# Multi-query attention on one core: last sum of VectorE's exponentials as accumulating DMAs of GpSimd, query loads by quarters of half batches, transpositions of 4096 columns

## The chip, the cores and the metric

One core of a Trainium2 chip. The core's engines are named as the profile names them: PE (TensorE, matmuls), ACT (ScalarE), DVE (VectorE), POOL (GpSimd), SP (SyncE, which here issues DMAs alone). Times are device microseconds (us). The metric is the time of one execution; the profile adds one execution's span and its instructions.

## The reference

```python
batch, seq_len, embed_dim = (8, 1024, 1024)
num_heads = 16
head_dim = embed_dim // num_heads          # 64
# q: (8, 1024, 16, 64)   k, v: (8, 1024, 64), all float32
q = q.transpose(0, 2, 1, 3)
scores = np.matmul(q, k.transpose(0, 1, 3, 2)) / np.sqrt(head_dim)
weights = np.exp(scores - np.max(scores, axis=-1, keepdims=True))
weights = weights / np.sum(weights, axis=-1, keepdims=True)
attn_out = np.matmul(weights, v)           # back to (8, 1024, 16, 64)
```

The 16 heads of a batch share its keys and values. The kernel takes no maximum off: it takes exponentials of the scaled scores and divides at the end by their sum, which a column of ones beside the values yields.

## The kernel before

**Tiles.** Work goes by pairs of heads: 8 batches x 8 pairs = 64 pairs (`NP`). Each pair has 8 tiles (`NKT`), one per 128 keys: a tile holds the scores of 128 keys against 1024 queries of two heads, so 128 x 2048. There are 512 tiles. Scores come in two halves of 512 queries, 128 x 1024 in float32, in one of three PSUM slots. `score` (L369) makes a half with two matmuls out of the transposed keys `k2t` and the transposed queries `qt`.

**Exponentials.** Most halves go to ACT: `exp_act` (L384), one instruction for 128 x 1024, written as fp16 into the weight tile `wt` (28 buffers). The other tiles go to DVE, by `exp_dve` (L389): two instructions (L396, one a half) turn the scores into 16-bit integers `z`, which read as fp16 are a first approximation of the exponential; then six steps over all 2048 columns refine it with a polynomial of the mantissa bits:

1. `f` = `z` and 1023 (L411)
2. `m` = (`f` - 1024) / 1024 (L413)
3. a linear factor out of `f`, kept in `wt` (L416)
4. `m` = `f` x `m` (L419)
5. `wt` = `m` x `wt`, the correction (L420)
6. `wt` = `z` + `wt`, as integers (L421)

**Values.** `value` (L424) multiplies a weight tile, as 128 x 128 stationary blocks, with the values of its 128 keys and a column of ones. The 16 blocks of a pair are in three groups (`GROUPS`), each summed over its 8 tiles in a PSUM bank; `reciprocal` and `normalise` (L443, L448) divide by the sum on DVE and issue the store of a pair on SP.

**Order.** `plan` (L50) lays out all instructions of PE, ACT and DVE in one list ahead of time, with a price for each kind of instruction and a due time for each tile. It decides which tiles are DVE's (a new one is taken when the DVE work in its list is under `BACKLOG`), and when the values of a tile can be multiplied. `LAG` says how many pairs the value matmuls stay behind the scores, `LAST` how many of the last tiles DVE takes none of. The three engines run in exactly that order; each waits, in its order, for what it needs. SP's and POOL's queues are not in the list: a scheduler orders them when the kernel is built, and each runs its own queue in order.

**Loads.** POOL loads the queries of a pair with a cast to fp16 (`load_q`, L307: 128 partitions x 8 runs of 128 elements, runs of 512 B at the source) into `qn` (4 buffers), keys and values a batch ahead (`load_k`, `load_v`). SP transposes by DMA: 1024 columns a pair (`trans_q`, L317) into `qt` (3 buffers), and the doubled keys of a batch (`trans_k`, L300). `begin(w)` (L469) issues these when the scores of pair w begin: the load of pair w+3, the transposition of pair w+2, and the next batch's keys at the third and values at the fifth pair of a batch. A load waits until the buffer that it overwrites has been transposed; a transposition waits until PE has made the last scores out of the `qt` buffer it overwrites. The first pair of all is loaded, cast and turned by other engines (`load_first`, `cast_first`, `turn_first`).

Of the kernel before, what the change touches and what calls it, by code (L numbers as in the profile page):

```python
# [9 lines left out]
FP32 = mybir.dt.float32  # L10
FP16 = mybir.dt.float16
U16 = mybir.dt.uint16
EXP = mybir.ActivationFunctionType.Exp
ALU = mybir.AluOpType
ENG = mybir.EngineType

P = 128
ONE = 1024.0
GA = 0.30457565
# [5 lines left out]
END, END_LAG, B_END = 5.0, 0.0, 5.0  # L25
VEC = dict(z=1.13, rec=0.11, norm=0.44)
STEPS = (0.6, 0.6, 0.6, 1.13, 1.13, 1.13)
VEC_L = 0.19
VEC_DEP = 0.12
GROUPS = ((0, 6), (6, 11), (11, 16))  # L30
# [1 line left out]
PITCH = 68  # L32
BACKLOG, BACK_END, BACK_LAST = 5.5, 3.0, 6.0
FIRST, DVE_0 = 4, 2.3
LAST = 12
WBUFS = 28
LAG = 1.8
FAR = 1e9

def follows(x, y):  # L40
# [9 lines left out]
def plan(NP, NKT):  # L50
# [28 lines left out]
    while p < NP or groups:  # L79
# [113 lines left out]
        else:  # L193
# [8 lines left out]
            if z:  # L202
                x = z[0]
                zs.remove(x)
                r, s, u = x
                T = max(T, r)
                emit(T, "z", *u)
                dve = T + VEC["z"]
                slot[s] = dve + VEC_L
                if u[1] == 1:  # L210
                    steps += [(u[0], n) for n in range(len(STEPS))]
                last = ("z", u[0])
            elif what == "ev":
                evs.remove(x)
                _, ep, eg, a, k = x
                emit(T + late, k, ep, eg)
                dve = T + late + VEC[k]
                if k == "norm":
                    acc[a] = dve + VEC_L
                last = x  # L220
            elif what == "step":
                steps.remove(x)
                emit(T + late, "step", *x)
                dve = T + late + STEPS[x[1]]
                if x[1] == len(STEPS) - 1:
                    ready[x[0]] = dve + VEC_L
                last = x
            else:
                nxt = [x[0] for x in zs + evs if x[0] > T] + [pe + 1e-6] * (pe > T)
                dve = max(min(nxt, default=0.0), T + 1e-3)  # L230
                last = None
# [6 lines left out]
def kernel(  # L238
# [12 lines left out]
    NQC = S // QC  # L251
    HT = NKT // NQC
    HP = H // 2
    NP = B * HP
    VW = 72
    vscale = ONE / (math.log(2.0) * math.sqrt(D))
# [17 lines left out]
    qt: dict = {}  # L274
    sc: dict = {}
    wt: dict = {}
    zs: dict = {}
    steps: dict = {}
    acc: dict = {}
    rec: dict = {}  # L280
# [2 lines left out]
    def load_k(b):  # L283

        st = kst.setdefault(b, {})
        st["k16"] = kvp.tile([P, NKT, 2, D], FP16, tag="k16", name=f"k16{b}")
        for r in range(2):
            nc.gpsimd.dma_start(  # L288
                out=st["k16"][:, :, r, :], in_=k[b].rearrange("(c p) d -> p c d", p=P)
            )  # L290

    def load_v(b):
        st = kst[b]
        st["v"] = kvp.tile([P, NKT, VW], FP16, tag="v", name=f"v{b}")
        nc.gpsimd.dma_start(  # L295
            out=st["v"][:, :, 0:D], in_=v[b].rearrange("(c p) d -> p c d", p=P)
        )
        nc.gpsimd.memset(st["v"][:, :, D : D + 1], 1.0)

    def trans_k(b):  # L300
# [3 lines left out]
            out=st["k2t"], in_=st["k16"].rearrange("p c r d -> p (c r d)")  # L304
        )

    def load_q(p):  # L307
        if p >= NP or p in qn:
            return
        b, hp = divmod(p, HP)  # L310
        qn[p] = qp.tile([P, NKT, 2 * D], FP16, tag="qn", name=f"qn{p}")
        nc.gpsimd.dma_start(  # L312
            out=qn[p],
            in_=q[b, :, 2 * hp : 2 * hp + 2, :].rearrange("(c p) h d -> p c (h d)", p=P),
        )

    def trans_q(p):  # L317
        if p >= NP:
            return
        qt[p] = qtp.tile([P, NKT + 1, P], FP16, tag="qt", name=f"qt{p}")[:, 0:NKT, :]  # L320
        nc.sync.dma_start_transpose(
            out=qt[p], in_=qn[p].rearrange("p c x -> p (c x)")
        )

    def load_first():

        st = kst.setdefault(0, {})
        st["kn"] = osbp.tile([P, NKT, D], FP32, tag="osb", name="kn")
        st["qf"] = osbp.tile([P, NKT, 2 * D], FP32, tag="osb", name="qf")
        for c in range(NQC):  # L330
            x = slice(HT * c, HT * c + HT)
            nc.sync.dma_start(
                out=st["kn"][:, x, :], in_=k[0].rearrange("(c p) d -> p c d", p=P)[:, x, :])
# [6 lines left out]
        qn[0] = qp.tile([P, NKT, 2 * D], FP16, tag="qn", name="qn0")  # L340
        qt[0] = qtp.tile([P, NKT + 1, P], FP16, tag="qt", name="qt0")[:, 0:NKT, :]

    def cast_first(c):
        st = kst[0]
        x = slice(HT * c, HT * c + HT)
        for r in range(2):
            nc.vector.tensor_copy(out=st["k16"][:, x, r, :], in_=st["kn"][:, x, :])  # L347
        if c == 0:
            nc.scalar.copy(out=qn[0][:, x, :], in_=st["qf"][:, x, :])  # L349
        else:  # L350
            nc.vector.tensor_copy(out=qn[0][:, x, :], in_=st["qf"][:, x, :])

    def turn_first(c):
        st = kst[0]
        x = slice(HT * c, HT * c + HT)
        kps = psp.tile([P, HT, P], FP16, tag="acc0", name=f"kps{c}")
        qps = psp.tile([P, HT, P], FP16, tag="acc1", name=f"qps{c}")
        for i in range(HT):
            nc.tensor.transpose(  # L359
                kps[:, i, :], st["k16"][:, HT * c + i, :, :].rearrange("p r d -> p (r d)"), ident)  # L360
        nc.vector.tensor_copy(out=st["k2t"][:, x, :], in_=kps)  # L361
        for i in range(HT):
            nc.tensor.transpose(qps[:, i, :], qn[0][:, HT * c + i, :], ident)
        if c == 0:
            nc.scalar.copy(out=qt[0][:, x, :], in_=qps)
        else:
            nc.vector.tensor_copy(out=qt[0][:, x, :], in_=qps)

    def score(t, c, s):  # L369
        p, j = divmod(t, NKT)  # L370
        sc[t, c] = psp.tile([P, 2, QC], FP32, tag=f"sc{s}", name=f"sc{t}_{c}")
        for h in range(2):
            nc.tensor.matmul(  # L373
                sc[t, c][:, h, :],
                kst[p // HP]["k2t"][64 * h : 64 * h + 64, j, :],
                qt[p].rearrange("p c x -> p (c x)")[
                    64 * h : 64 * h + 64, c * QC : (c + 1) * QC
                ],
                start=True, stop=True, tile_position=(64 * h, 0),
            )  # L380
        if t not in wt:
            wt[t] = wtp.tile([P, 2, S], FP16, tag="wt", name=f"wt{t}")
# [6 lines left out]
    def exp_dve(t, c):  # L389


        name = f"{t}"
        if c == 0:
            zs[t] = dvp.tile([P, 2, S], U16, tag="z", bufs=3, name=f"z{name}")
        z = zs[t]
        nc.vector.tensor_scalar(  # L396
            out=z[:, :, c * QC : (c + 1) * QC], in0=sc.pop((t, c)), scalar1=vscale,
            scalar2=15 * ONE, op0=ALU.mult, op1=ALU.add,
        )
        if c == 0:  # L400
            return
        w = wt[t]
        V = nc.vector
        x: dict = {}

        def new(key, dtype):
            x[key] = dvp.tile([P, 2, S], dtype, tag=key, name=f"{key}{name}")
            return x[key]

        steps[t] = (  # L410
            lambda: V.tensor_scalar(  # L411
                out=new("f", U16), in0=z, scalar1=1023, scalar2=None, op0=ALU.bitwise_and),
            lambda: V.tensor_scalar(  # L413
                out=new("m", FP16), in0=x["f"], scalar1=-ONE, scalar2=1.0 / ONE,
                op0=ALU.add, op1=ALU.mult),
            lambda: V.tensor_scalar(  # L416
                out=w, in0=x["f"], scalar1=GB / ONE, scalar2=GA,
                op0=ALU.mult, op1=ALU.add),
            lambda: V.tensor_tensor(out=x["m"], in0=x["f"], in1=x["m"], op=ALU.mult),  # L419
            lambda: V.tensor_tensor(out=w, in0=x["m"], in1=w, op=ALU.mult),  # L420
            lambda: V.tensor_tensor(out=w.bitcast(U16), in0=z, in1=w, op=ALU.add),  # L421
        )

    def value(p, grp, j, n, s):  # L424
# [42 lines left out]
    begun = 0  # L467

    def begin(w):  # L469
        load_q(w + 3)  # L470
        trans_q(w + 2)
        b, hp = divmod(w, HP)
        if b + 1 < B:
            if hp == 2:
                load_k(b + 1)
            if hp == 4:
                load_v(b + 1)
            if hp == HP - 3:
                trans_k(b + 1)
# [2 lines left out]
    load_q(1)  # L482
    load_v(0)
    load_q(2)
    trans_q(1)
    with tc.manual_schedule(engines={ENG.PE, ENG.Activation, ENG.DVE}):
        cast_first(0)
# [51 lines left out]
```

## Time and profile before

| What | Value |
|---|---|
| three runs | 795.47, 796.89, 797.02 us; median 796.89 |
| the profiled execution's time | 795.15 us |
| its span | 793.4 us |
| TensorE clock granted, share of full | 0.991 |
| tiles of DVE / halves of ACT | 87 / 850 |
| DMA, mean | 93 GB/s, 73.60 MB |
| first exponential of ACT begins | 7.25 us |
| first value matmul begins | 27.32 us |

A row of instructions has its line, engine and operation, what it writes from what, shapes and count; behind the bar the busy time in us, the mean of one in ns, and the engine's idle time just before them with what ended most of it. Neighbours on one engine overlap a little, so means can add up to more than the busy time. A queue's row has packets, MB and the share of the span of 16 DMA engines that the packets took. A row of DMA issues ends with the median time from issue to landing. A row of waits has who waited, for whom, us in total, how often, and the longest.

Not shown again below: the stretch from 60 to 740 us is even. In windows of 200 us there ACT is busy 200.00 of 200 us, DVE 195.6 to 195.9, PE 171.8 to 172.0, with a DMA share of 0.59 to 0.63. In the first 20 us ACT is busy 15.23 us and the DMA share is 1.29 (packets in flight together count each); in the last 23.4 us ACT is busy 17.83.

### The profile page before, as it was taken

Reading aid. Unit: us, or ns where it says so; the run is one execution under the profiler, and the core shown is the slowest. Engines: PE = TensorE matmul, PEld = TensorE weight load, DVE = VectorE, ACT = ScalarE, POOL = GpSimd, SP = SyncE. Lnnn points to the kernel's source line nnn. Section 1 sums busy time; section 2 is a strip of 40 time slices with the busy share of each in tenths; the row PEclk is TensorE's granted clock in tenths of the full one; section 3 lists DMA queues with packets and bytes.
Section 4 is the critical chain, followed back from the end, with each engine's and each line's share of the span. In section 5 each row is a group of like instructions: output and inputs, shape, how many; then the busy total and the mean of one; then the engine's idle time right before and its main releaser. Section 6 shows DMA issues by size and latency. Waiting matters only on the chain.

```text
span 793.4 us, 23419 instructions
## 1 busy us (share of the span) xinstructions
PE 671.1 (85%) x10256; PEld 414.6 (52%) x10256; DVE 762.7 (96%) x1088; ACT 782.1 (99%) x853; POOL 79.1 (10%) x99
## 2 busy tenths in 40 slices
PE   5888888888888888888888888888888888888886
PEld 1355555555555555555555555555555455555555
DVE  6999999999999999999999999999999999999996
ACT  7999999999999999999999999999999999999997
POOL 5200011100100001010010000000010000000000
PEclk9799999999999999999999999999999999999999
DMA  9954685545865449656485445765555745552322
GB/s 148 114 99 68 107 117 79 105 70 95 120 86 97 82 80 121 99 83 101 65 130 91 78 95 95 94 101 81 95 107 70 114 74 89 101 92 55 76 56 81
DMA packets 231110, 73.60 MB, mean 93 GB/s; under 512 B 164448, under 2 KB 231008, under 8 KB 231008
## 3 DMA queue, kind: packets, MB, share of 16 engines
q1 hardware_dynamic: 141024, 51.92, 30.8%
q0 software_dynamic: 88400, 19.40, 27.6%
q8 instruction: 80, 1.31, 0.7%
q10 hardware_dynamic: 1584, 0.79, 0.4%
q14 instruction: 22, 0.18, 0.1%
HBM read 39.58 MB, written 33.55 MB: 92 GB/s over the span
## 4 chain that ended last, share of the span: by engine, by line
ACT 74%; PE 9%; issue 9%; DVE 6%; DMA 0%; ACTq 0%
ACT wt L385 74%; PE sc L373 5%; PE acc L437 4%; DVE z L396 2%; DVE m L419 1%; DVE wt L420 1%; DVE osb L453 1%; DVE wt L416 1%; DMA kn<-in_k_dram 0%; DVE rec L446 0%; DVE wt L421 0%; DVE f L411 0%; DVE m L413 0%; DVE k L347 0%; PE kps L359 0%
## 5 line engine op out<-in xcount | busy, mean ns | idle before, releaser
L385 ACT ACTIVATE wt<-sc 128x1024 f16<-128x1024 f32 x850 | 779.6, 1291 | 1.7 <-PE sc L373 1.7
L373 PE MATMUL sc<-qt,k2t 64*128 64x512 f16 x2048 | 372.3, 385 | 112.4 <-ACT wt L385 91.3
L437 PEld LDWEIGHTS <-wt 128*128 128x128 f16 x8192 | 281.5, 98 | 141.5 <-issue 139.8
L437 PE MATMUL acc<-v,wt 128*128 128x65 f16 x8192 | 352.7, 194 | 0.0
L373 PEld LDWEIGHTS <-k2t 64*128 64x128 f16 x2048 | 131.6, 93 | 226.3 <-issue 167.0
L396 DVE TENSOR_SCALAR z<-sc 128x1024 uint16<-128x1024 f32 x174 | 212.2, 1220 | 17.3 <-PE sc L373 14.9
L312 POOL DMA_DIRECT2D qn<-in_q_dram x63 | 57.1, 907 | 579.1 <-DMA qt<-qn 578.8
L419 DVE TENSOR_TENSOR m<-f,m 128x2048 f16<-128x2048 uint16 x87 | 104.8, 1205 | 0.0
L420 DVE TENSOR_TENSOR wt<-m,wt 128x2048 f16<-128x2048 f16 x87 | 104.5, 1202 | 0.3
L421 DVE TENSOR_TENSOR wt<-z,wt 128x2048 uint16<-128x2048 uint16 x87 | 104.7, 1203 | 0.0
L453 DVE TENSOR_TENSOR osb<-acc,rec 128x320 f32<-128x320 f32 (+1 forms) x192 | 96.6, 503 | 0.2
L413 DVE TENSOR_SCALAR m<-f 128x2048 f16<-128x2048 uint16 x87 | 60.4, 695 | 0.5
L411 DVE TENSOR_SCALAR f<-z 128x2048 uint16<-128x2048 uint16 x87 | 59.7, 686 | 0.1
L416 DVE TENSOR_SCALAR wt<-f 128x2048 f16<-128x2048 uint16 x87 | 58.5, 672 | 0.0
L446 DVE RECIPROCAL rec<-acc 128x5 f32<-128x5 f32 (+1 forms) x192 | 34.9, 183 | 2.2 <-PE acc L437 2.1
L288 POOL DMA_DIRECT2D k<-in_k_dram x14 | 13.3, 957 | 10.4 <-DMA k2t<-k 10.4
L295 POOL DMA_DIRECT2D v<-in_v_dram x8 | 7.2, 895 | 36.6 <-PE acc L437 32.1
L359 PE MATMUL kps<-ident,k 128*128 128x128 f16 x8 | 1.2, 308 | 4.8 <-DVE k L347 4.8
L347 DVE CAST k<-kn 128x256 f16<-128x256 f32 x4 | 1.2, 336 | 4.0 <-DMA kn<-in_k_dram 4.0
L359 PEld LDWEIGHTS <-k 128*128 128x128 f16 x8 | 0.7, 131 | 5.6 <-DVE k L347 4.8
L349 ACT ACT_TABLE_LOAD x1 | 1.3, 1283 | 1.9 <-issue 1.9
L361 DVE COPY k2t<-kps 128x512 f16<-128x512 f16 x2 | 0.8, 425 | 2.3 <-PE kps L359 2.3
(13 smaller groups left out, 6.2 us busy)
## 6 DMA issues: line engine op xcount, KB each, us to landing
out_dram<-osb SPq DMA_DIRECT2D x63, 512.0 KB, 3.5
qn<-in_q_dram POOLq DMA_DIRECT2D x63, 256.0 KB, 4.3
k<-in_k_dram POOLq DMA_DIRECT2D x14, 128.0 KB, 4.3
v<-in_v_dram POOLq DMA_DIRECT2D x8, 128.0 KB, 4.6
qt<-qn SPq DMA_TRANSPOSE x63, 3.6
qf<-in_q_dram ACTq DMA_DIRECT2D x2, 256.0 KB, 4.4
kn<-in_k_dram SPq DMA_DIRECT2D x2, 128.0 KB, 3.7
out_dram<-osb SPq DMA_DIRECT2D x1, 256.0 KB, 2.4
```

The source lines that it names most:

```text
L312: nc.gpsimd.dma_start(out=qn[p], in_=q[b, :, 2 * hp : 2 * hp + 2, :].rearrange("(c p) h d -> p c (h d)", p=P),)
L373: nc.tensor.matmul(sc[t, c][:, h, :], kst[p // HP]["k2t"][64 * h : 64 * h + 64, j, :], qt[p].rearrange("p c x -> p (c x)")[64 * h : 64 * h ...
L385: nc.scalar.activation(out=wt[t][:, :, c * QC : (c + 1) * QC], in_=sc.pop((t, c)), func=EXP, scale=ascale)
L396: nc.vector.tensor_scalar(out=z[:, :, c * QC : (c + 1) * QC], in0=sc.pop((t, c)), scalar1=vscale, scalar2=15 * ONE, op0=ALU.mult, op1=ALU.add,
L411: lambda: V.tensor_scalar(out=new("f", U16), in0=z, scalar1=1023, scalar2=None, op0=ALU.bitwise_and),
L413: lambda: V.tensor_scalar(out=new("m", FP16), in0=x["f"], scalar1=-ONE, scalar2=1.0 / ONE, op0=ALU.add, op1=ALU.mult),
L416: lambda: V.tensor_scalar(out=w, in0=x["f"], scalar1=GB / ONE, scalar2=GA, op0=ALU.mult, op1=ALU.add),
L419: lambda: V.tensor_tensor(out=x["m"], in0=x["f"], in1=x["m"], op=ALU.mult),
L420: lambda: V.tensor_tensor(out=w, in0=x["m"], in1=w, op=ALU.mult),
L421: lambda: V.tensor_tensor(out=w.bitcast(U16), in0=z, in1=w, op=ALU.add),
L437: nc.tensor.matmul(acc[p, grp][:, x - lo, 0 : D + 1], w[:, h, i * P : (i + 1) * P], kst[p // HP]["v"][:, j, 0 : D + 1], start=(n == 0 and ...
L453: nc.vector.tensor_tensor(out=osb[p][:, lo:hi, :], in0=acc.pop((p, grp))[:, 0 : hi - lo, 0:D], in1=rec.pop((p, grp))[:, 0 : hi - lo].unsqu ...
```

## The change

**The sixth step.** Step 1's source `z` is now written straight into the weight tile (`wt` read as uint16), so there is no `z` buffer. Steps 3 and 5 write a buffer of their own, `l` (4 buffers): the factor as fp16, then the correction as int16. For all DVE tiles but those among the last 24 (`LATE`), the sixth step is no instruction of DVE: POOL issues a DMA from `l` onto `wt` that adds as it writes (`accum_op`). In the plan such a tile has five steps, and its values are due `ADD_L` = 9 us after the fifth. With `LAST` = 14 and `LAG` = 2.0 the list holds 98 DVE tiles, 95 of them with an addition by DMA, and 828 halves of ACT.

**Queries.** A group is four pairs, half of a batch. From the second group on, `load_part` loads a quarter of the rows of a group for all its four pairs: 128 partitions x 2 runs of 512 elements, 2 KB runs at the source. A group has four such loads and one transposition of 4096 columns (`trans_half`). `qn` and `qt` have 2 buffers of four pairs each. The pairs 1 to 3 are loaded and transposed one by one as before. `score` reads the queries of a pair out of the group's tile with a stride (`queries`).

**Keys and values** are laid out with 8 consecutive keys on a partition, where before keys 128 apart were; both in the same way. The values of the next batch are loaded at the sixth pair of a batch, before it was the fifth.

**Queues.** As built, POOL issues 180 DMAs where it issued 85, and SP transposes 25 times where it did 70. POOL's first addition stands behind 21 loads: three queries of single pairs, twelve quarter loads, and the keys and values of the first batches. Later, in twelve places, quarter loads of a group stand ahead of an addition, at seven of them all four loads of a group.

```diff
+ADD_L, LATE = 9.0, 24
-LAST = 12
+LAST = 14
-LAG = 1.8
+LAG = 2.0
...
-                    steps += [(u[0], n) for n in range(len(STEPS))]
+                    steps += [(u[0], n) for n in range(len(STEPS) - (u[0] < NT - LATE))]
...
-                if x[1] == len(STEPS) - 1:
-                    ready[x[0]] = dve + VEC_L
+                if all(y[0] != x[0] for y in steps):
+                    ready[x[0]] = dve + VEC_L + ADD_L * (x[0] < NT - LATE)
...
-    qp = ctx.enter_context(tc.tile_pool(name="qp", bufs=4))
-    qtp = ctx.enter_context(tc.tile_pool(name="qtp", bufs=3))
+    qp = ctx.enter_context(tc.tile_pool(name="qp", bufs=2))
+    qtp = ctx.enter_context(tc.tile_pool(name="qtp", bufs=2))
...
-            out=st["v"][:, :, 0:D], in_=v[b].rearrange("(c p) d -> p c d", p=P)
+            out=st["v"][:, :, 0:D], in_=v[b].rearrange("(p c) d -> p c d", p=P)
...
+    def place_q(g):
+        qn[g] = qp.tile([P, QP * NKT, P], FP16, tag="qn", name=f"qn{g}")
+        qt[g] = qtp.tile([P, QP * NKT + 1, P], FP16, tag="qt", name=f"qt{g}")[:, 0 : QP * NKT, :]
...
+    def load_part(g, i):
+        if g * QP >= NP:
+            return
+        if i == 0:
+            place_q(g)
+        b, r = divmod(g, 2)
+        c = slice(2 * i, 2 * i + 2)
+        nc.gpsimd.dma_start(
+            out=qn[g].rearrange("p (c n) x -> p c (n x)", n=QP)[:, c, :],
+            in_=q[b, :, 2 * QP * r : 2 * QP * (r + 1), :].rearrange(
+                "(c p) h d -> p c (h d)", p=P)[:, c, :],
+        )
+
+    def trans_half(g):
+        if g * QP >= NP:
+            return
+        nc.sync.dma_start_transpose(out=qt[g], in_=qn[g].rearrange("p b x -> p (b x)"))
+
+    def queries(p, c):
+        g, n = divmod(p, QP)
+        if g == 0:
+            x = of_pair(qt[g], n)
+        else:
+            x = qt[g].rearrange("p (c n) x -> p c n x", n=QP)[:, :, n, :]
+        return x[:, NKT // 2 * c : NKT // 2 * (c + 1), :]
...
-        if c == 0:
-            zs[t] = dvp.tile([P, 2, S], U16, tag="z", bufs=3, name=f"z{name}")
-        z = zs[t]
+        z = wt[t].bitcast(U16)
...
+        def correct():
+            r = x["l"].bitcast(I16)
+            V.tensor_tensor(out=r, in0=x["m"], in1=x["l"], op=ALU.mult)
+            if t < NKT * NP - LATE:
+                nc.gpsimd.dma_start(
+                    out=z.rearrange("p h x -> p (h x)"), in_=r.rearrange("p h x -> p (h x)"),
+                    accum_op=ALU.add,
+                )
...
-            lambda: V.tensor_scalar(
-                out=w, in0=x["f"], scalar1=GB / ONE, scalar2=GA,
+            lambda: V.tensor_scalar(
+                out=new("l", FP16, 4), in0=x["f"], scalar1=GB / ONE, scalar2=GA,
                 op0=ALU.mult, op1=ALU.add),
             lambda: V.tensor_tensor(out=x["m"], in0=x["f"], in1=x["m"], op=ALU.mult),
-            lambda: V.tensor_tensor(out=w, in0=x["m"], in1=w, op=ALU.mult),
-            lambda: V.tensor_tensor(out=w.bitcast(U16), in0=z, in1=w, op=ALU.add),
+            correct,
+            lambda: V.tensor_tensor(out=z, in0=z, in1=x["l"].bitcast(I16), op=ALU.add),
...
     def begin(w):
-        load_q(w + 3)
-        trans_q(w + 2)
+        if w == 0:
+            for i in range(QP):
+                load_part(1, i)
+            trans_q(2)
+            trans_q(3)
+        if w % QP == 2:
+            trans_half(w // QP + 1)
+        if w > 1:
+            load_part((w - 2) // QP + 2, (w - 2) % QP)
         b, hp = divmod(w, HP)
         if b + 1 < B:
             if hp == 2:
                 load_k(b + 1)
-            if hp == 4:
+            if hp == 5:
                 load_v(b + 1)
```

More of the change, by code (lines that the diff above doesn't have):

```diff
@@ L12 @@
 U16 = mybir.dt.uint16
+I16 = mybir.dt.int16
 EXP = mybir.ActivationFunctionType.Exp
@@ L253 @@
     HP = H // 2
+    QP = HP // 2
     NP = B * HP
@@ L276 @@
     wt: dict = {}
-    zs: dict = {}
     steps: dict = {}
@@ L288, in load_k @@
             nc.gpsimd.dma_start(
-                out=st["k16"][:, :, r, :], in_=k[b].rearrange("(c p) d -> p c d", p=P)
+                out=st["k16"][:, :, r, :], in_=k[b].rearrange("(p c) d -> p c d", p=P)
             )
@@ L305, in trans_k, with of_pair @@
         )
+    def place_q(g):
+        qn[g] = qp.tile([P, QP * NKT, P], FP16, tag="qn", name=f"qn{g}")
+        qt[g] = qtp.tile([P, QP * NKT + 1, P], FP16, tag="qt", name=f"qt{g}")[:, 0 : QP * NKT, :]
+    def of_pair(x, n):
+        return x[:, NKT * n : NKT * (n + 1), :]
     def load_q(p):
[L308 to L311, printed above, removed]
         nc.gpsimd.dma_start(
-            out=qn[p],
-            in_=q[b, :, 2 * hp : 2 * hp + 2, :].rearrange("(c p) h d -> p c (h d)", p=P),
+            out=of_pair(qn[0], p),
+            in_=q[0, :, 2 * p : 2 * p + 2, :].rearrange("(c p) h d -> p c (h d)", p=P),
         )
     def trans_q(p):
-        if p >= NP:
-            return
-        qt[p] = qtp.tile([P, NKT + 1, P], FP16, tag="qt", name=f"qt{p}")[:, 0:NKT, :]
-        nc.sync.dma_start_transpose(
-            out=qt[p], in_=qn[p].rearrange("p c x -> p (c x)")
-        )
+        nc.sync.dma_start_transpose(
+            out=of_pair(qt[0], p), in_=of_pair(qn[0], p).rearrange("p c x -> p (c x)")
+        )
+    def load_part(g, i):
+        if g * QP >= NP:
+            return
+        if i == 0:
[6 more added lines that the diff above has]
+                "(c p) h d -> p c (h d)", p=P)[:, c, :],
+        )
+    def trans_half(g):
[9 more added lines that the diff above has]
+        return x[:, NKT // 2 * c : NKT // 2 * (c + 1), :]
     def load_first():
@@ L332, in load_first @@
             nc.sync.dma_start(
-                out=st["kn"][:, x, :], in_=k[0].rearrange("(c p) d -> p c d", p=P)[:, x, :])
+                out=st["kn"][:, x, :], in_=k[0].rearrange("(p c) d -> p c d", p=P)[:, x, :])
             nc.scalar.dma_start(
@@ L339, in load_first @@
         st["k2t"] = kvp.tile([P, NKT + 1, P], FP16, tag="k2t", name="k2t0")[:, 0:NKT, :]
-        qn[0] = qp.tile([P, NKT, 2 * D], FP16, tag="qn", name="qn0")
-        qt[0] = qtp.tile([P, NKT + 1, P], FP16, tag="qt", name="qt0")[:, 0:NKT, :]
+        place_q(0)
     def cast_first(c):
@@ L348, in cast_first @@
         if c == 0:
-            nc.scalar.copy(out=qn[0][:, x, :], in_=st["qf"][:, x, :])
+            nc.scalar.copy(out=of_pair(qn[0], 0)[:, x, :], in_=st["qf"][:, x, :])
         else:
-            nc.vector.tensor_copy(out=qn[0][:, x, :], in_=st["qf"][:, x, :])
+            nc.vector.tensor_copy(out=of_pair(qn[0], 0)[:, x, :], in_=st["qf"][:, x, :])
     def turn_first(c):
@@ L362, in turn_first @@
         for i in range(HT):
-            nc.tensor.transpose(qps[:, i, :], qn[0][:, HT * c + i, :], ident)
+            nc.tensor.transpose(qps[:, i, :], of_pair(qn[0], 0)[:, HT * c + i, :], ident)
         if c == 0:
-            nc.scalar.copy(out=qt[0][:, x, :], in_=qps)
+            nc.scalar.copy(out=of_pair(qt[0], 0)[:, x, :], in_=qps)
         else:
-            nc.vector.tensor_copy(out=qt[0][:, x, :], in_=qps)
+            nc.vector.tensor_copy(out=of_pair(qt[0], 0)[:, x, :], in_=qps)
     def score(t, c, s):
@@ L373, in score @@
             nc.tensor.matmul(
-                sc[t, c][:, h, :],
+                sc[t, c][:, h, :].rearrange("p (i x) -> p i x", x=P),
                 kst[p // HP]["k2t"][64 * h : 64 * h + 64, j, :],
-                qt[p].rearrange("p c x -> p (c x)")[
-                    64 * h : 64 * h + 64, c * QC : (c + 1) * QC
-                ],
+                queries(p, c)[64 * h : 64 * h + 64, :, :],
                 start=True, stop=True, tile_position=(64 * h, 0),
@@ L389, in exp_dve @@
     def exp_dve(t, c):
-        name = f"{t}"
-        if c == 0:
-            zs[t] = dvp.tile([P, 2, S], U16, tag="z", bufs=3, name=f"z{name}")
-        z = zs[t]
+        z = wt[t].bitcast(U16)
         nc.vector.tensor_scalar(
@@ L401, in exp_dve, with new @@
             return
-        w = wt[t]
         V = nc.vector
         x: dict = {}
-        def new(key, dtype):
-            x[key] = dvp.tile([P, 2, S], dtype, tag=key, name=f"{key}{name}")
+        def new(key, dtype, bufs):
+            x[key] = dvp.tile([P, 2, S], dtype, tag=key, bufs=bufs, name=f"{key}{t}")
             return x[key]
+        def correct():
[6 more added lines that the diff above has]
+                )
         steps[t] = (
             lambda: V.tensor_scalar(
-                out=new("f", U16), in0=z, scalar1=1023, scalar2=None, op0=ALU.bitwise_and),
+                out=new("f", U16, 2), in0=z, scalar1=1023, scalar2=None, op0=ALU.bitwise_and),
             lambda: V.tensor_scalar(
-                out=new("m", FP16), in0=x["f"], scalar1=-ONE, scalar2=1.0 / ONE,
+                out=new("m", FP16, 2), in0=x["f"], scalar1=-ONE, scalar2=1.0 / ONE,
                 op0=ALU.add, op1=ALU.mult),
             lambda: V.tensor_scalar(
-                out=w, in0=x["f"], scalar1=GB / ONE, scalar2=GA,
+                out=new("l", FP16, 4), in0=x["f"], scalar1=GB / ONE, scalar2=GA,
                 op0=ALU.mult, op1=ALU.add),
             lambda: V.tensor_tensor(out=x["m"], in0=x["f"], in1=x["m"], op=ALU.mult),
-            lambda: V.tensor_tensor(out=w, in0=x["m"], in1=w, op=ALU.mult),
-            lambda: V.tensor_tensor(out=w.bitcast(U16), in0=z, in1=w, op=ALU.add),
+            correct,
+            lambda: V.tensor_tensor(out=z, in0=z, in1=x["l"].bitcast(I16), op=ALU.add),
         )
@@ L484 @@
     load_q(2)
+    load_q(3)
     trans_q(1)
```

## The prediction

> **What bounds the kernel now.** I read the busy shares first, then the chain of waits, the groups of instructions, the DMA queues, the waits, and last one stretch of the timeline.
>
> ```profile
> PE 671.1 (85%) x10256; PEld 414.6 (52%) x10256; DVE 762.7 (96%) x1088; ACT 782.1 (99%) x853; POOL 79.1 (10%) x99
> ...
> ACT 74%; PE 9%; issue 9%; DVE 6%; DMA 0%; ACTq 0%
> ...
> L385 ACT ACTIVATE wt<-sc 128x1024 f16<-128x1024 f32 x850 | 779.6, 1291 | 1.7 <-PE sc L373 1.7
> L373 PE MATMUL sc<-qt,k2t 64*128 64x512 f16 x2048 | 372.3, 385 | 112.4 <-ACT wt L385 91.3
> L396 DVE TENSOR_SCALAR z<-sc 128x1024 uint16<-128x1024 f32 x174 | 212.2, 1220 | 17.3 <-PE sc L373 14.9
> L419 DVE TENSOR_TENSOR m<-f,m 128x2048 f16<-128x2048 uint16 x87 | 104.8, 1205 | 0.0
> L420 DVE TENSOR_TENSOR wt<-m,wt 128x2048 f16<-128x2048 f16 x87 | 104.5, 1202 | 0.3
> L421 DVE TENSOR_TENSOR wt<-z,wt 128x2048 uint16<-128x2048 uint16 x87 | 104.7, 1203 | 0.0
> L413 DVE TENSOR_SCALAR m<-f 128x2048 f16<-128x2048 uint16 x87 | 60.4, 695 | 0.5
> L411 DVE TENSOR_SCALAR f<-z 128x2048 uint16<-128x2048 uint16 x87 | 59.7, 686 | 0.1
> L416 DVE TENSOR_SCALAR wt<-f 128x2048 f16<-128x2048 uint16 x87 | 58.5, 672 | 0.0
> ```
>
> ACT runs exponentials back to back (99%, 1.7 us idle before 850 of them), DVE is 96% busy doing the other 174, and PE waits for ACT (91.3 us). So time is exponentials of ACT times their pace, 779.6/850 = 0.917 us (the mean of 1291 ns overlaps its neighbour). DVE could take more of them only if each cost it less. The groups also give DVE's price of one tile: two z at 1.22, three cheap steps, three products or sums at 1.20 each.
>
> ```profile
> q1 hardware_dynamic: 141024, 51.92, 30.8%
> q0 software_dynamic: 88400, 19.40, 27.6%
> ...
> out_dram<-osb SPq DMA_DIRECT2D x63, 512.0 KB, 3.5
> qn<-in_q_dram POOLq DMA_DIRECT2D x63, 256.0 KB, 4.3
> k<-in_k_dram POOLq DMA_DIRECT2D x14, 128.0 KB, 4.3
> ...
> qt<-qn SPq DMA_TRANSPOSE x63, 3.6
> ...
> POOL qn L312 <- DMA qt<-qn: 578.8, 57, 16.1
> ...
> POOL v L295 <- PE acc L437: 32.1, 5, 8.2
> ...
> SPq L321 <- PE sc L373: 415.3, 57, 12.8
> ```
>
> These are the queues, the issues with their time to landing, and the waits. POOL's queue stands still for 579 us, because each query load waits for a transposition to leave its buffer, and that transposition (on SP) waits for PE to finish the scores of an old pair. Today nobody is behind those loads. In the changed kernel the additions are.
>
> ```profile
> 12.88 1.17 POOL L312 DMA_DIRECT2D qn<-in_q_dram  x1 [7.58 <-DMA qt<-qn]
> ...
> 13.60 0.94 DVE L413 TENSOR_SCALAR m<-f 128x2048 f16<-128x2048 uint16 x1
> ```
>
> In the timeline a DVE step beside a POOL issue takes 0.94 us, where its group's mean is 0.695.
>
> **The change part by part.** *Division of work.* The planner's list now has 98 DVE tiles for 87, and 828 exponentials on ACT for 850. ACT saves 22 x 0.917 = 20.2 us.
>
> *DVE.* z: 22 more x 1.22 = +26.8. Five steps: 11 more x (0.686 + 0.695 + 0.672 + 1.205 + 1.202 = 4.46) = +49.1. Last sum: 84 fewer (87 to 3) x 1.203 = -101.1. In all -25.2, so DVE is busy some 738 us for 763: 95% of a span shorter by 20. It stays just off the bound, as now. The fifth step now writes int16. No row has that; L419 to L421 mix f16 and uint16 and take 1.202 to 1.205 whatever the type. The other end is one element at the pace of z, 1024 in 1.22, so 2.4 for 2048, which adds 98 x 1.2 = 118 us. I take 1.2. PE keeps its instructions; 20 us less still leaves it over 90 of its 112 us idle.
>
> *The addition's cover.* An addition reads 512 KB twice and writes it once; no row shows one. Lower end: the output store of 512 KB, 3.5 us from issue to landing. Upper end: the query load's 0.9 us of issue and 3.4 us of the rest, the rest doubled for double the bytes (it reads 512 KB and writes 256): 7.7. I take 5.5, the middle. In the changed kernel's order 11 to 16 exponentials of ACT (median 12) stand between a tile's fifth step and the first value matmul that reads it: 10.1 to 14.7 us, less 1.2 for the step itself, so 8.9 to 13.5. The addition is hidden in 8.9 even at 7.7, where POOL's queue is free. Uncovered it would hold PE's fixed order, and with it ACT's next score tile: each us late beyond the score tile or so held ready is a us lost. POOL issues 180 DMAs for 85; 95 x 0.9 = 86 us more still leaves it under a quarter busy.
>
> The Trainium skill's page SBUF — State Buffer (section SBUF: two separate sides, its box on DMAs that VectorE blocks, with the figures under A bandwidth-pool intuition that's wrong) speaks against this. A DMA of GpSimd needs descriptors that GpSimd cannot write while VectorE runs a two-port step, and a 620 ns transfer becomes 3100. Here POOL's issues beside a DVE 96% busy take 0.9 us and land in 4.3, which shows no such size. By the page's difference, 2.5 us on each addition, 8.0 would still be under 8.9, and the places below would lose more.
>
> *POOL beside DVE.* 95 more issues; the pair of rows above shows 0.25 us on a step that overlaps one. If a third of them hit a step, 8 us of DVE; its idle 30 us mostly takes it. From 0 to 8, I take 1.
>
> *Queries and transpositions.* 60 quarter loads (2 KB runs) replace 60 of 512 B runs: fewer packets, so no more than the 0.9 and 4.3 of today. One transposition now does four: lower end 3.6 + 3 x 1.24 (SP's issue of one, 1.24 us in its tile's view) = 7.3; upper end 4 x 3.6 = 14.4. I take 7.3, since transpositions on one queue overlap today. There are 25 for 70, as many bytes. The new layout of keys and values permutes the keys and costs nothing. The value load's 32.1 us of waits would now hold additions; it is issued one pair later, and the longest wait, 8.2 us, is less than a pair (16 score tiles less DVE's three, 13 x 0.917 = 12).
>
> *The step that can hurt.* From the fourth group of four pairs on, a group's first quarter load waits for the transposition of the buffer it takes, which waits for the last scores of two groups earlier; POOL's order puts an addition behind it, twelve times in the run. Behind the transposition at those places: one load at five, four at seven (with two key loads at three of these). From those last scores to the value matmul that needs the addition there are 17 to 20 exponentials at the five places (15.6 to 18.3 us) and 19 to 25 at the seven (17.4 to 22.9). Needed: 7.3 + 0.9 + 5.5 = 13.7 at the five, 7.3 + 3.6 + 5.5 = 16.4 at four of the seven and 18.2 with key loads. The margins are 1.0 to 4.7 us, 34 in all over twelve places: met on paper, narrowly. The loads drain ahead of the addition in the same software queue, so I put 3 us in all (0 at the low end).
>
> *Start.* Twenty-one loads stand on POOL before the first addition, the last four behind the first long transposition. Query loads of today's kind are drained near 10.5 us (the transposition that releases POOL is done at 12.9); four quarter loads at 1.5 each bring 16.5, the transposition 24, four issues 27.5, the addition 33. ACT's first exponential is at 7.25 and 27 stand before the matmul that needs it: 32.0. Late by 1 on paper; in that burst I take 3, from 0 to 9.
>
> *Sum,* against the profiled execution's own 795.15 (span 793.4 and 1.8 around it): -20.2 + 1 + 3 + 3 = -13.2, so 782. The median of the runs shown, 796.89, stands 0.2% over that execution, so 784.
>
> **Rivals.** (1) *Part given back.* Transposition and addition together take 3 us more than taken; the twelve margins then leave 8.5 us late in all: 795.15 - 20.2 + 8.5 + 1 + 4 = 788.5, with the 0.2% 790. For: margins near 1 us at three places. Against: ACT's cushion.
> (2) *The additions late behind the transpositions: slower.* One POOL queue serves both. At 5 us more than taken the twelve places are late by 26 us, and 795.15 - 20.2 + 26 + 5 = 806. With both prices at their upper ends (9.3 more) it is 78 us late, some 858. It is slower from about 3.9 us on, where the lateness passes what is left of the 20. For: the 579 us that POOL spends behind transpositions today, and 7.8 us as the longest landing of one short transposition. Against: such landings are rare, median 3.6.
> (3) *The int16 product runs at half the pace:* 118 us more on DVE, some 900. Only its absence from the rows speaks for it.
> (4) *The long transposition relieves the queues,* and nothing is late, the start neither: 795.15 - 20.2 = 775, 776.5 by the median.
>
> **How the numbers follow.** Forecast with (4): 0.60, its own range 775 to 790. (1): 0.17, two thirds of it still faster by over 0.2% (1.6 us, about what a measurement tells from no change), the rest mostly within. (2): 0.20. (3): 0.03. Faster 0.71, within 0.04, slower 0.25. The range goes from 774 to 804: below it nothing is left but luck, above it the worse half of (2) and all of (3).
>
> **What would show it.** 828 exponentials at 0.917 or so and ACT at 98% say the division holds. DVE near 738 busy, the fifth step at 1.2. An addition from issue to landing of 3.5 to 7.7, the long transposition 7.3 to 14.4. PE's weight loads of the value matmul waiting for the addition's DMA: nearly none outside the start and the twelve places; more there is (1), over 20 us is (2). The forecast is wrong if additions beside other traffic take over 9 us, or if POOL's actual order of readiness is later than the order of exponentials says.

## The result and the profile after

| | median us | runs |
|---|---|---|
| before | 796.4 | 795.47 to 797.02, four |
| changed | 871.6 | 869.31 to 875.34, four |

The ratio is 1.095, 95% interval 1.094 to 1.097: slower, by 75 us, where 784 us, some 12 less, were forecast. In the experiments an execution over 1.5% above the fastest of its kernel is left out of medians and ratios; with all of them the medians of e3 and e9, which later expectations quote, are 808 and 835 us. The profiled execution took 872.91 us, its span is 871.0. From the page of the changed kernel: busy shares, the chain of waits, four groups and the DMA issues.

```profile
PE 677.4 (78%) x10256; PEld 408.5 (47%) x10256; DVE 741.0 (85%) x1081; ACT 767.7 (88%) x831; POOL 158.6 (18%) x194
...
ACT 38%; DMA 30%; PE 15%; issue 7%; DVE 6%; POOL 3%; SPq 0%; POOLq 0%; ACTq 0%; DVEq 0%
...
L414 ACT ACTIVATE wt<-sc 128x1024 f16<-128x1024 f32 x828 | 765.2, 1192 | 93.5 <-PE sc L404 93.0
...
L472 PE MATMUL acc<-v,wt 128*128 128x65 f16 x8192 | 348.1, 198 | 80.6 <-DMA wt<-l 80.5
...
L438 DVE TENSOR_TENSOR l<-m,l 128x2048 int16<-128x2048 f16 x98 | 118.8, 1212 | 0.0
...
L337 POOL DMA_DIRECT2D qn<-in_q_dram x60 | 46.1, 841 | 135.1 <-DMA qt<-qn 84.4
...
wt<-l POOLq DMA_DIRECT2D x95, 512.0 KB, 6.1
...
qn<-in_q_dram POOLq DMA_DIRECT2D x63, 256.0 KB, 7.2
k<-in_k_dram POOLq DMA_DIRECT2D x14, 128.0 KB, 10.0
...
qt<-qn SPq DMA_TRANSPOSE x18, 10.7
```

ACT's line accounts for the whole difference of the spans: its busy time fell by 14.4 us (779.6 to 765.2) and its idle time rose by 91.8 (1.7 to 93.5), together +77.4 of the 77.6. ACT waits for scores (L404); PE makes them in a fixed order and waits in it for an addition (`wt<-l`). The waits of the changed kernel say how often and how long at most:

```profile
ACT wt L414 <- PE sc L404: 93.0, 45, 13.1
...
PEld L472 <- DMA wt<-l: 86.1, 20, 13.4
...
PE acc L472 <- DMA wt<-l: 80.5, 19, 13.1
```

Nineteen waits, 4 us each on average: not every addition is late, a few are very late. One place of the twelve, in the timelines of SP, POOL and PE (start, length, what, and in brackets the idle time before it and its releaser):

```profile
233.88 7.66 SPq L346 DMA_TRANSPOSE qt<-qn  x1
...
248.64 2.88 POOL L337 DMA_DIRECT2D qn<-in_q_dram  x4 [8.67 <-DMA qt<-qn]
251.48 1.75 POOL L290 DMA_DIRECT2D k<-in_k_dram  x2
253.22 1.93 POOL L440 DMA_DIRECT2D wt<-l  x2
...
265.30 1.06 PE L472 MATMUL acc<-v,wt 128*128 128x65 f16 x16 [8.80 <-DMA wt<-l]
```

And the piece of the chain of waits that spans it (start, length, what):

```profile
253.22 12.03 DMA wt<-l
```

SP issues the long transposition at 233.9. POOL's first load can go at 248.6. Two additions stand behind six loads; the first is issued at 253.2, 7.4 us after its tile's fifth step ended, and lands 12.0 us later, where the median is 6.1. PE stands still for 8.8 us.

### The profile page after: what moved, and what is told of

It reads as the page before. It is cut to its first block, busy times and chain, and to the rows that moved or that the text cites. A ratio compares the mean times of both kernels' runs of the same rounds, so it can differ in the third digit from the quotient of the medians.

```text
span 871.0 us, 23608 instructions
## 1 busy us (share of the span) xinstructions
PE 677.4 (78%) x10256; PEld 408.5 (47%) x10256; DVE 741.0 (85%) x1081; ACT 767.7 (88%) x831; POOL 158.6 (18%) x194
## 4 chain that ended last, share of the span: by engine, by line
ACT 38%; DMA 30%; PE 15%; issue 7%; DVE 6%; POOL 3%; SPq 0%; POOLq 0%; ACTq 0%; DVEq 0%
ACT wt L414 38%; DMA wt<-l 16%; DMA qt<-qn 11%; PE acc L472 8%; PE sc L404 7%; POOL qn L337 2%; DVE wt L423 2%; DMA qn<-in_q_dram 2%; DVE m L454 1%; DMA k2t<-k 1%; DVE osb L488 1%; DVE l L438 1%; POOL k L290 1%; DVE l L451 0%; DVE m L448 0%
## 5 line engine op out<-in xcount | busy, mean ns | idle before, releaser
L414 ACT ACTIVATE wt<-sc 128x1024 f16<-128x1024 f32 x828 | 765.2, 1192 | 93.5 <-PE sc L404 93.0
L404 PE MATMUL sc<-qt,k2t 64*128 64x512 f16 x2048 | 377.3, 407 | 104.0 <-ACT wt L414 88.0
L472 PE MATMUL acc<-v,wt 128*128 128x65 f16 x8192 | 348.1, 198 | 80.6 <-DMA wt<-l 80.5
L472 PEld LDWEIGHTS <-wt 128*128 128x128 f16 x8192 | 290.5, 100 | 208.2 <-issue 120.1
L423 DVE TENSOR_SCALAR wt<-sc 128x1024 uint16<-128x1024 f32 x196 | 239.3, 1221 | 58.1 <-PE sc L404 56.7
L404 PEld LDWEIGHTS <-k2t 64*128 64x128 f16 x2048 | 116.5, 95 | 244.0 <-issue 194.8
L440 POOL DMA_DIRECT2D wt<-l x95 | 90.6, 955 | 495.6 <-ACT wt L414 170.0
L454 DVE TENSOR_TENSOR m<-f,m 128x2048 f16<-128x2048 uint16 x98 | 118.8, 1212 | 0.0
L438 DVE TENSOR_TENSOR l<-m,l 128x2048 int16<-128x2048 f16 x98 | 118.8, 1212 | 0.0
L337 POOL DMA_DIRECT2D qn<-in_q_dram x60 | 46.1, 841 | 135.1 <-DMA qt<-qn 84.4
L451 DVE TENSOR_SCALAR l<-f 128x2048 f16<-128x2048 uint16 x98 | 66.6, 679 | 0.0
L446 DVE TENSOR_SCALAR f<-wt 128x2048 uint16<-128x2048 uint16 x98 | 65.7, 682 | 0.1
L319 POOL DMA_DIRECT2D qn<-in_q_dram x3 | 2.9, 973 | 0.4 <-issue 0.4
## 6 DMA issues: line engine op xcount, KB each, us to landing
qt<-qn SPq DMA_TRANSPOSE x18, 10.7
```

The lines of the kernel that those rows point to most:

```text
L337: nc.gpsimd.dma_start(out=qn[g].rearrange("p (c n) x -> p c (n x)", n=QP)[:, c, :], in_=q[b, :, 2 * QP * r : 2 * QP * (r + 1), :].rearrang ...
L404: nc.tensor.matmul(sc[t, c][:, h, :].rearrange("p (i x) -> p i x", x=P), kst[p // HP]["k2t"][64 * h : 64 * h + 64, j, :], queries(p, c)[64 ...
L414: nc.scalar.activation(out=wt[t][:, :, c * QC : (c + 1) * QC], in_=sc.pop((t, c)), func=EXP, scale=ascale)
L423: nc.vector.tensor_scalar(out=z[:, :, c * QC : (c + 1) * QC], in0=sc.pop((t, c)), scalar1=vscale, scalar2=15 * ONE, op0=ALU.mult, op1=ALU.add,
L438: V.tensor_tensor(out=r, in0=x["m"], in1=x["l"], op=ALU.mult)
L440: nc.gpsimd.dma_start(out=z.rearrange("p h x -> p (h x)"), in_=r.rearrange("p h x -> p (h x)"), accum_op=ALU.add,)
```

## The experiments

Each ran beside the kernel before. Times are medians; ratios are to the kernel before, with the 95% interval. Idle time of ACT is that of L414 or its counterpart.

### Is it the additions, or the queries?

```diff
# e1_no_adds
-ADD_L, LATE = 9.0, 24
+ADD_L, LATE = 9.0, 512
# e4_reverse
-                    out=z.rearrange("p h x -> p (h x)"), in_=r.rearrange("p h x -> p (h x)"),
+                    out=r.rearrange("p h x -> p (h x)"), in_=z.rearrange("p h x -> p (h x)"),
```

> LATE = 512: every tile of VectorE keeps its sixth step on VectorE, none is added by a DMA; the planner then gives VectorE 86 tiles and ACT 852 halves. Quarter loads, long transpositions, the new layout of keys and values, LAG 2.0 and LAST 14 stay. Theory A (the additions stand in POOL's queue behind quarter loads that wait for a long transposition, and drain behind them): without additions nobody waits for that queue, 852 x 0.917 plus 15 = 796 us, ACT idle a few us. Rival B (each addition is too slow by itself): 796 as well. Rival C (the query part: long transpositions, strided reads of the queries, a lower clock of TensorE) makes the loss: 860 or more, ACT idle as long as in the changed kernel.

> The changed kernel with each addition the other way round: the DMA adds z onto the buffer of the correction, so that the weight tile keeps the uncorrected approximation (the sixth step's result does not reach the values) and PE waits for no DMA. The same bytes, issues, queue order and holds remain. Theories A and B both: PE's wait for additions is the whole loss, 776 to 790 us, ACT idle under 15 us. Rival C, or DMA traffic that slows the engines by itself: 830 or more.

Measured: e1 797.3 us, 1.0015 (1.0006 to 1.0024); e4 780.9 us, 0.9815 (0.9778 to 0.9852). These are ACT's row and the issue row of the reversed additions in the profile of e4:

```profile
L414 ACT ACTIVATE wt<-sc 128x1024 f16<-128x1024 f32 x828 | 760.4, 1256 | 3.2 <-PE sc L404 3.1
...
l<-wt POOLq DMA_DIRECT2D x95, 512.0 KB, 7.7
```

With the same DMAs in the same queues, even slower to land (7.7), but with nobody on PE waiting for them, the kernel gains 15 us and ACT idles 3.2. So PE's wait for the additions is the loss. Of the 20 us by division of work 19 are there in ACT's busy time (762.9 for 782.1) and 15 in the time. The query part alone costs nothing that matters; rival C falls.

### Is every addition too slow, or do some stand behind something?

```diff
# e3_pool_order
-    with tc.manual_schedule(engines={ENG.PE, ENG.Activation, ENG.DVE}):
+    with tc.manual_schedule(engines={ENG.PE, ENG.Activation, ENG.DVE, ENG.Pool}):
# e2_old_queries: qn, qt, load_q, trans_q, begin and the layouts of the kernel before;
# plan, exp_dve, LAG, LAST and the later value load of the changed one
```

> The additions and their plan (98 tiles, 828 halves) with the queries of the kernel before: one load and one transposition of 1024 columns a pair, four qn and three qt buffers, old layout of keys and values. Theory A: one load waits for one short transposition (3.6 us) before an addition, so each hold is short but there are some 60 of them: 780 to 810 us, longest landing of an addition under 10 us. Rival B: 860 or more. Rival C: 776 to 785, since the query part alone is to blame.

> The changed kernel's instructions, but POOL's queue runs in the order in which the program names them, as PE, ACT and DVE do: a quarter load a pair, between additions, four pairs after the transposition that it waits for was put in SP's queue; the first addition stands behind 8 loads and not 21. Theory A: no addition is held, so the 22 exponentials saved show: 776 to 790 us, ACT idle under 15 us, landings of additions 4.5 to 8 us with no 13. Rival B: still 850 or more, with PE waiting for additions all along. Rival C: 850 or more, but PE waits for something other than additions.

Measured: e3 806.0 us, 1.014 (1.011 to 1.016); e2 828.4 us, 1.039 (1.033 to 1.045). Both missed what theory A expected. In e2 the holds are not short: POOL's loads wait 188.8 us for transpositions, 32 times and up to 17.3 us. POOL's order alone gives back 66 of the 75 us, so rival B falls: the same additions are not too slow by themselves. But 806 is not 780: something else makes some late. I took it to be the transposition of 4096 columns, which shares the DMA engines with an addition (theory A2), and tried order and length apart.

### Order of the queues, and length of the transposition

```diff
# e6_short_turns, e8_short_turns_auto (e8: this alone; e6: with POOL's and SP's queues in program order)
-        nc.sync.dma_start_transpose(out=qt[g], in_=qn[g].rearrange("p b x -> p (b x)"))
+        x = slice(NKT * i, NKT * (i + 1))
+        nc.sync.dma_start_transpose(
+            out=qt[g][:, x, :], in_=qn[g][:, x, :].rearrange("p b x -> p (b x)")
+        )
...
-        if w % QP == 2:
-            trans_half(w // QP + 1)
+        trans_part(w // QP + 1, w % QP)
# e9_sp_order, e12_long_turns: the changed kernel with both queues in program order
+... ENG.DVE, ENG.Pool, ENG.SP}):
# e10_half_turns: as e6, two transpositions of 2048 columns
# e5_old_queries_order: e2_old_queries with POOL's queue in program order
```

> The changed kernel with POOL's and SP's queues in program order, and each transposition of 4096 columns cut into four of 1024, one a pair, each for the quarter loaded two pairs earlier. Same plan, same additions, same loads, same bytes. Theory A2: 776 to 790 us, ACT idle under 12 us. Rival D: 805 or more.

> Only the cut into four short transpositions, with both queues as the scheduler orders them. Theory A2: the loads on POOL still stand ahead of additions and wait for transpositions, so most of the loss stays: 825 to 865 us. Rival E (the long transposition alone does the harm, by its length): 776 to 800.

> POOL's and SP's queues in program order, transpositions of 4096 columns as in the changed kernel. Theory A2: no load is held, but the long transposition still runs beside additions: 797 to 815, as with POOL's order alone (808), some additions landing after 12 us or more. Rival F (it was SP's order, stores and transpositions bunched, and not the length): 776 to 790.

> e9_sp_order once more, beside the others: both queues in program order, one transposition of 4096 columns. By theory A2 805 to 850 us, clearly over e10_half_turns.

> As e6_short_turns (780.6 us, four transpositions of 1024 columns), but two of 2048. Theory A2, by the length: between 781 and the 808 to 835 of one of 4096 in the same order, 785 to 812; ACT idle 12 to 45 us. If length is not what matters: 778 to 783.

> The additions with the old per-pair loads and short transpositions (as in e2_old_queries, 828 us), and POOL's queue in program order. Theory A2 (two holds: loads on POOL that wait for a transposition, and a long transposition that shares the DMA engines with an addition): neither is left, 776 to 792 us, additions land within 10 us. Rival D (any transposition, load or store beside an addition makes it late; the DMA engines are too full for 9 us of cover): 805 or more, as POOL's order alone gave 808.

| order of the queues | 4096 columns | 2 x 2048 | 4 x 1024 |
|---|---|---|---|
| the scheduler's | changed kernel 871.6 | | e8 879.8, 1.105 (1.103 to 1.107) |
| POOL by the program | e3 806.0, 1.014 (1.011 to 1.016) | | |
| POOL and SP by the program | e9 828.9, 1.041 (1.036 to 1.046); e12 830.0, 1.041 (1.035 to 1.047) | e10 792.1, 0.994 (0.991 to 0.997) | e6 780.6, 0.980 (0.976 to 0.984) |

And e5 791.2, 0.992 (0.989 to 0.995), with the old per-pair loads and POOL by the program.

The row at the bottom is a dose and its answer: the same loads and additions, the same rule of order, and 780.6, 792.1, 830 or so as the transposition grows. The cut ones also stand at several pairs of a group, so length and spacing change together. The column at the right says that order matters by itself: 879.8 against 780.6; e2 and e5 say it too, 828.4 against 791.2. Neither remedy alone is enough. e8 came out above what theory A2 gave it (825 to 865), and e9 above its 797 to 815; e5, e6, e10 and e12 lie in their ranges. PE's value matmuls in e8:

```profile
L475 PE MATMUL acc<-v,wt 128*128 128x65 f16 x8192 | 345.5, 198 | 89.3 <-DMA wt<-l 85.5
```

Three rows of e6 (ACT, PE's value matmuls, quarter loads) and its transpositions:

```profile
L417 ACT ACTIVATE wt<-sc 128x1024 f16<-128x1024 f32 x828 | 761.2, 1227 | 8.1 <-PE sc L407 7.9
...
L475 PE MATMUL acc<-v,wt 128*128 128x65 f16 x8192 | 335.2, 195 | 3.2 <-DMA wt<-l 2.3
...
L337 POOL DMA_DIRECT2D qn<-in_q_dram x60 | 74.6, 1246 | 0.3 <-issue 0.2
...
qt<-qn SPq DMA_TRANSPOSE x63, 7.7
```

PE waits 2.3 us for additions in the whole run, and POOL never for a transposition. In e12 the loads wait as little, but the long transposition lands in 14.7, and PE waits 39 us:

```profile
L472 PE MATMUL acc<-v,wt 128*128 128x65 f16 x8192 | 339.4, 196 | 39.6 <-DMA wt<-l 39.1
...
L337 POOL DMA_DIRECT2D qn<-in_q_dram x60 | 73.9, 1234 | 0.3 <-issue 0.2
...
qt<-qn SPq DMA_TRANSPOSE x18, 14.7
```

e9 against e3 is not settled: putting SP's stores and transpositions in program order too made the kernel with long ones some 23 us slower, and why stays open.

### Loads that wait, or loads that come in a burst?

```diff
# e11_burst, against e6_short_turns
-        if w > 1:
-            load_part((w - 2) // QP + 2, (w - 2) % QP)
+        if w % QP == 2:
+            for i in range(QP):
+                load_part((w - 2) // QP + 2, i)
```

> As e6_short_turns, but the four quarter loads of a group are issued one after the other, at the pair where the first of them was issued; none waits for a transposition. It tells the burst (four loads drain ahead of an addition in POOL's queue) from the hold (loads that wait). Theory burst: 4 x 1.8 us of loads and 3 of the addition and 2 to land, 12 us against 9 of cover: 795 to 830 us, longest landing 12 or more. Theory hold: 778 to 790.

Measured: 861.3 us, 1.081 (1.078 to 1.085): above the range of the burst theory, and far from the hold's. The one edit, four loads at once and none of them waiting, costs 81 us against e6. In the timeline of e11 (POOL) at one such burst:

```profile
332.40 3.10 POOL L337 DMA_DIRECT2D qn<-in_q_dram  x4
335.40 2.06 POOL L290 DMA_DIRECT2D k<-in_k_dram  x2
339.94 0.89 POOL L443 DMA_DIRECT2D wt<-l  x1 [2.48 <-PE sc L407]
```

Its chain of waits there:

```profile
339.94 21.76 DMA wt<-l
```

And the groups of its value matmuls and quarter loads on the page:

```profile
L475 PE MATMUL acc<-v,wt 128*128 128x65 f16 x8192 | 345.7, 198 | 74.9 <-DMA wt<-l 74.3
...
L337 POOL DMA_DIRECT2D qn<-in_q_dram x60 | 50.6, 1102 | 0.0
```

The addition is issued 2.5 us after the last load, alone, and lands 21.8 us later. In the packet records of that stretch the four quarter loads run from 336 to 344 (1.8 us each, not the 0.8 of their issue); the keys' packets follow, nine tenths of them begun by 346.4 and the last at 357. The addition's first packet begins at 344.7, 4.8 us after its issue, and its last ends 14.8 us later, beside a store and a short transposition that lands after 21.0 us where the median is 7.5. So the burst is enough; the loads here wait for nothing (0.0 idle before them). But more than the queue ahead of the addition is at work.

The trace lets the way of each addition that PE waited for be split: from the end of its fifth step to POOL's issue (the hold), from there to its first packet (the queue and POOL's own work), from the first packet to the last, and from there to landing. Packets are counted off in order, 128 to an addition, so the split is approximate where two additions overlap. Means in us:

| kernel | additions PE waited for | to issue | to first packet | first to last packet | to landing |
|---|---|---|---|---|---|
| changed | 19 | 4.5 | 5.2 | 4.0 | 1.1 |
| e8 | 16 | 6.1 | 5.6 | 3.6 | 1.0 |
| e11 | 13 | 0.6 | 6.0 | 7.9 | 1.3 |
| e12 | 10 | 0.7 | 5.9 | 8.2 | 0.9 |
| all additions of the changed kernel, median | | 0.6 | 2.5 | 3.3 | 0.4 |

In the scheduler's order (changed, e8) the loss is hold and queue, and the transfers run at nearly their usual pace. With the queues in program order no addition is issued over 1.4 us after its fifth step: e11 and e12 lose by the queue and by transfers of more than twice the usual length. So e11 shows that a burst does harm without any hold; it does so in part by another way than the changed kernel.

The page DMA: Bandwidth & Descriptors of the Trainium skill (section Queues, rings and completion order) has descriptors of one queue consumed in order on each DMA engine (said there of the queues of SP and ACT), and queues taken in turn by packets. The first agrees with e11's queue of POOL, where the addition's first packet begins (344.7) after the last quarter load's last has ended (343.8). The same page's Rules for kernel authors advise one large transfer in place of many small ones. In this case four transpositions of 256 KB did better than one of 1 MB, 780.6 against 830 us: here it counts when the additions land.

### A longer cover

```diff
# e7_short_turns_add11, against e6_short_turns
-ADD_L, LATE = 9.0, 24
+ADD_L, LATE = 11.0, 24
```

> As e6_short_turns, with ADD_L = 11: the plan puts 2 us more between the fifth step and the values (99 tiles, 826 halves). 826 x 0.917 + 15 = 772 if the rest of ACT's 11 us idle came from additions that were late by under 2 us and the 28 weight buffers suffice: 772 to 779. If the buffers bind: 782 or more.

Measured: 826.6 us, 1.034 (1.027 to 1.040), a miss on the bad side. PE waits only 12.5 us for additions there; ACT idles 37.5 us in some 40 mostly short gaps, one addition took 18.9 us, and TensorE's granted clock is 0.915 where e6 has 0.964. The plan changes throughout with this number (other tiles on DVE, 28 weight buffers to hold for longer); which of it costs the time stays open.

## Why the prediction was wrong

- **Bound and division of work: right.** DVE was to be busy 738 us and was 741.0; the int16 product was taken at 1.2 and took 1.212, so rival 3 fell. The gain of 20.2 us with nothing late gave 776.5, and e4 and e6, in which little or nothing waits, gave 780.9 and 780.6.
- **The addition by itself: right at the median.** 5.5 us was taken from issue to landing, between 3.5 and 7.7. The 60 additions issued with no load of POOL's in flight have a median of 5.3. Five of them took over 9 us, up to 10.8; all five were issued within 1.1 us after a long transposition, and PE waited 4.7 us for four of them, which the prediction had at nothing. The 35 issued behind loads in flight have a median of 10.1. In all 27 of 95 took over 9 us, the sign of a wrong forecast that the prediction had named.
- **"The step that can hurt": wrong, and it decided.** The places and their order were right, twelve of them and the start. The lateness of the twelve was put at 3 us in all, on margins of 1.0 to 4.7; PE's waits for additions at them add up to 62.7 us. At the place shown, one with key loads, 18.2 us were said to be needed from the transposition's issue to the addition's landing; it took 265.3 - 233.9 = 31.4, of which 4.6 for issuing the loads, less than the 5.4 taken. Two terms were too small:
  - the transposition, taken at its lower end of 7.3 us: the median is 10.6 to 10.7, up to 14.2, and POOL's first load at this place went after 14.8;
  - the addition behind the loads: 12.0 here, up to 13.5, where 5.5 was taken. The loads were priced by their issue (0.9 each) and not by their drain. A quarter load takes 0.74 to issue, but in a row they land 1.5 us apart at the median, and four of them and two key loads stood ahead. "The loads drain ahead of the addition in the same software queue" was written down and given no price at these places, though the prediction's own start has a quarter load drain in 1.5.
- **The start: outside its bounds.** The first addition was to be late by 3 us, 0 to 9. ACT's wait there is 13.1 us, the longest of the run: the addition was issued at 35.2 and not near 28, and took 10.6 to land.
- **Rival 2 was the case,** mechanism and place, and with both prices at their upper ends it was put at 858. That this comes near 871.6 is partly luck: it has 78 us at the twelve places, where PE waited 62.7, and the start, the four other additions and ACT's idle time of 93.0 beyond PE's 80.5 make up for it. The rival was given 0.20, because the sum took the lower end of the transposition and the middle of the addition, each as if alone on the DMA engines. At the place shown they come together: the transposition, the loads it releases and the additions that have piled up meanwhile all run in the same 31 us.
- **The skill's page weighed there,** SBUF — State Buffer on VectorE blocking GpSimd's DMAs: POOL's issue of an addition took 0.955 us on average, 1.9 at most, beside a DVE 85% busy (0.984 in e6, with DVE 95% busy), and where no load was in flight it landed after 5.3, against an estimate of 5.5. The page's 2.5 us more is not visible here either; no run has additions beside an idle DVE.

## What to carry to other kernels

A DMA on which compute waits must not share an in-order queue with bulk loads that can arrive in a burst: price such loads by what they drain, not by what they take to issue, and add up everything that one event releases. Where a scheduler orders a queue, write its order out once something urgent is in it; here the same instructions went from 879.8 to 780.6 us. Beside urgent transfers, and with both queues in program order, several short transpositions beat one long one; in the scheduler's order they did not (879.8 against 871.6). e6 is faster than both kernels, at 0.980 of the kernel before (0.976 to 0.984).

## What the runs showed of the hardware that was not expected

- An addition's packets of 4096 B took 0.328 us when alone (median 0.335 in the changed kernel), eight on each of 16 engines, so 2.6 us for 512 KB. In e12 there were additions whose packets took up to 5.8 us each and whose transfer lasted 7 to 13 us, at the long transpositions, which landed there after up to 37.6 us; in the changed kernel no transfer lasted over 5.8. So the long transposition harms in two ways: an addition that runs beside it is stretched (e12), and where the scheduler put loads behind it, it lets them out late and all at once (the changed kernel). A long transposition is not needed for the stretch: in e11, with transpositions of 1024 columns, transfers behind bursts lasted up to 15.5 us, with packets of up to 6.4. What makes single packets so slow no run shows.
- A quarter load, with a quarter of the packets (1024 B after the cast, 0.098 us each), takes less engine time than the old load's 256 B ones (0.041 each): 16 x 0.098 = 1.6 us against 64 x 0.041 = 2.6 for the same bytes.
- TensorE's granted clock fell where PE stood still. After the wait that ended at 265.3 it was 0.50 of full from 260 to 270 us, and 1.00 from 210 to 256 and from 271 to 314; over the span it was 0.914 against 0.991 before. PE's busy time does not follow it: 677.4 us in the changed kernel, 677.1 in e1 at a clock of 0.999, 652.5 in e4 at 0.972, for the same matmuls. No run separates what the lower clock adds to the stalls.
